# GpSimd makes two of the four sums of weights in gate and up's seven-product units; this stage's other transfers on SP's queue

## The chip, the cores and the metric

The kernel runs on one core of one Trainium2 chip. The metric is the time of one execution on the device in microseconds (us). Before the change it is 1453.75 us, the median of three runs (1453.46 to 1453.94).

The engines are TensorE (PE in the profile), VectorE (DVE), ScalarE (ACT), GpSimd (POOL) and SyncE (SP). Each runs its own instructions in order and waits for others by semaphores. DMA transfers are issued from an engine's queue: here SP's and POOL's, but for a few.

## What is computed

One encoder layer in float32, for 256 rows of 2048 features: four mixers side by side behind one input projection (gated linear attention, a Fourier mixer, a long convolution, a short convolution), an output projection, a cross-attention over 256 memory rows, and a gated feed-forward layer. The change is in the last:

```python
def swiglu(h, w_gate_up, w_down):
    gate, up = jnp.split(h @ w_gate_up, 2, axis=-1)
    return (jax.nn.silu(gate) * up) @ w_down

x = x + swiglu(rms_norm(x, norm_g[l, 2]), w_gate_up[l], w_down[l])
return rms_norm(x, final_norm_g)
```

`w_gate_up` is 2048 by 11264, `w_down` 5632 by 2048.

## The kernel before

**Weights.** All weights come as one stream of 252 slabs of 1 MB (128 partitions by 2048 columns, which are sixteen 128 by 128 blocks). `Stream.raw` (L129) loads a slab into a `raw` tile from SP's queue (L136); in gate and up there are four such tiles in turn, so that a load waits until the slab four before it has been read. To keep float32's accuracy a product is made of three matmuls of a shorter format. For that `Stream.split` (L150) divides 1024 columns at a time: ACT copies the rounded weights to `wh` (L156), DVE subtracts them from the raw ones and leaves the rest in `wl` (L157). A pair of `wh` and `wl` is called a part here. `Stream.free` (L141) allows five parts at a time in this stage (pools `wp` and `wp2`); the next part's copy waits until PE is through with the oldest one.

**A product** is `Block.part` (L494): the three matmuls of L495 (`wh` by the rounded activations), L496 (`wl` by them) and L497 (`wh` by their rest), each of 512 columns, into a PSUM bank (`pg` or `pm`).

**Gate and up** (`gate_up`, L956) loops over eleven blocks j of 512 hidden columns, and in each over eight slabs i. A slab holds two rows of blocks k (2i and 2i + 1) for gate and for up. A plain slab is two parts and eight products. Slabs 1, 3 and 5 (in block 0 slab 5 alone; `sevens`, L53) are units: seven products make what eight would (Strassen's scheme in Winograd's form), with sums of weights on one side and sums of activations, made beforehand by `left` (L966), on the other. That is 31 units in this stage. The down projection has twelve more.

**A unit's weights** are made in four parts by `Stream.make` (L161). With b11, b12, b22, b21 for the four 512-column quarters of the raw slab:

- part 0: split b11 (512 columns); then one DVE instruction of 1024 columns (L189, called through `op`) puts b11 - b12 and b22 - b12 in the places of b11 and b12;
- part 1: split b22 and b21 as loaded; then two DVE instructions of 512 columns: b22 becomes b22 + (b11 - b12), and b21 becomes b21 less the new b22;
- part 2: split the first two quarters (the sums of part 0);
- part 3: split the last two quarters (the sums of part 1).

Each sum is written into the raw tile in place. `keep` after each part (`keep_place`, L345) ties every instruction of it to the one before on the same engine, so that the scheduler can't move it past others. Parts are made ahead of their use, as far as buffers are free (`look`, L204).

**Other work of the stage.** `combine` (L995) adds a unit group's banks to the sums kept in SBUF, `finish` (L1009) adds the plain products, applies the gate and has `store_turned` (L520) transpose the result on DVE (L525) and store it to a scratch tensor `hidden` in HBM with four DMAs each (L530), eight in a block. `fetch` (L932) loads 128 hidden columns back at a time (L941) and splits them for the down projection: 16 during gate and up (`form` is None), 28 more in the down projection, where some are also formed into sums. `turn` (L1067) transposes the residual on DVE (16 times, L1074), stores it with 64 DMAs (L1077) and loads it with 8 (L1081). All these DMAs (L530, L941, L1077, L1081) are issued from POOL's queue.

**Order.** A list scheduler fixes each engine's order from the order in which the program is written down and the dependencies. The small work (`combine`, `finish`, `turn`, `fetch`) is written down by generators of the class `Background` (L244), which counts PE time (`pe`) and a debt of DVE time (`dve`, L262) in the program: `poll` lets a generator go on only while the debt is under 0.9 us.

Of the kernel before, what the change touches and what calls it, by code (L numbers as in the profile page):

```python
# [18 lines left out]
ALU = mybir.AluOpType  # L19
# [3 lines left out]
P = 128  # L23
# [88 lines left out]
class Stream:  # L112
# [48 lines left out]
    def make(self):  # L161

        nc, (slab, part) = self.nc, self.todo
        n = 16 * slab + 8 * part
        if n >= NBLK - HELD:
            parts = [(self.places.pop(0)) for _ in range(2)]
            r = self.raw(slab)[:, part * 1024:part * 1024 + 1024]
            for a, (wh, wl) in zip((0, 512), parts):
                nc.scalar.copy(wh, r[:, a:a + 512])
                nc.vector.tensor_tensor(out=wl, in0=r[:, a:a + 512], in1=wh.bitcast(F32), op=ALU.subtract)  # L170
            self.bg.dve(1024, 2)
            self.items.append((None, parts))
            self.todo = (slab + part, 1 - part)
            return True
        pool = self.free(slab)
        if pool is None:
            return False
        raw = self.raw(slab)
        at = 48 if any(a <= n < b for a, b in ROWS) else 8
        r = raw[:, part % 2 * 1024:part % 2 * 1024 + 1024]  # L180
        if not seven(slab):
            mark = len(nc.cur_bb.bb.instructions)
            self.split(pool, at, r, [0, 256, 512, 1024] if n == 0 else [0, 512, 1024] if n == 8 else [0, 1024])
            if DOWN <= slab < DOWN + 2 * AHEAD:
                self.keep(mark)
            self.todo = (slab + part, 1 - part)
            return True
        mark = len(nc.cur_bb.bb.instructions)
        op = lambda out, a, b, what=ALU.subtract: nc.vector.tensor_tensor(out=out, in0=a, in1=b, op=what)  # L189
        self.split(pool, at, r, [0, 512] if part == 0 else [0, 1024])  # L190
        b11, b12, b22, b21 = (raw[:, a:a + 512] for a in range(0, 2048, 512))
        if part == 0:
            blk = raw.rearrange("p (b c) -> p b c", b=4)
            op(r.rearrange("p (b c) -> p b c", b=2), blk[:, 0:3:2, :], blk[:, 1:2, :].to_broadcast([P, 2, 512]))
            self.bg.dve(1024)
        elif part == 1:
            op(b22, b22, b11, ALU.add)
            op(b21, b21, b22)
            self.bg.dve(1024, 2)
        self.keep(mark)  # L200
        self.todo = (slab + part // 3, (part + 1) % 4)
        return True
# [87 lines left out]
class Block:  # L290
# [226 lines left out]
                    self.bg.poll()  # L517
        return ps

    def store_turned(self, to, u, src, keep=False):  # L520

        nc = self.nc
        self.bg.dve(src.shape[1])
        mark = self.mark()
        nc.vector.transpose(u, src)  # L525
        if keep:
            self.keep_place(mark)
        to = to.rearrange("(b f) t -> f b t", f=32)
        for a in range(4):
            nc.gpsimd.dma_start(to[:, :, 32 * a:32 * a + 32],  # L530
                                u[32 * a:32 * a + 32, :].rearrange("f (b t) -> f b t", t=32))


# [398 lines left out]
    def fetch(self, f, ks, ahead, pause, form=None):  # L932

        m = {}
        for n in range(len(ks) + ahead):
            if n < len(ks):
                k = ks[n]
                while len(self.stored) <= k // 4:
                    yield
                m[k] = self.tmp()  # L940
                self.nc.gpsimd.dma_start(m[k], self.ff[k * P:(k + 1) * P, :])  # L941
            if n >= ahead:
                i = ks[n - ahead]
                if i >= PLAIN:
                    if i % 2:
                        form(i - 1, m.pop(i - 1), m.pop(i))
                        self.have += 2
                        yield 3.0
                    continue
                mark = self.mark()  # L950
                self.split(f[i], m.pop(i))
                self.keep_place(mark)
                self.have += 1
                yield pause

    def gate_up(self, sw, gp, f):  # L956
# [52 lines left out]
        def finish(j, cs, s):  # L1009
# [5 lines left out]
            for r in range(2):  # L1015
                g, h = s[r]
                self.tt(h, cs[r][1], h, ALU.add)
                yield SOON
            for r in range(2):
                g, h = s[r]  # L1020
                u = gp.tile([P, 512], F32, name="u", tag="u", bufs=2)
                self.stt(h, h, box["col"][:, r:r + 1], g, ALU.mult, ALU.mult)
                yield SOON
                self.store_turned(self.ff[j * 512:(j + 1) * 512, r * P:(r + 1) * P], u, h)
                yield SOON
            self.stored.append(j)

# [39 lines left out]
    def turn(self):  # L1067
# [3 lines left out]
        for i in range(16):  # L1071
# [2 lines left out]
            nc.vector.transpose(u, self.resk(i))  # L1074
            for a in range(4):
                c = i * P + 32 * a
                nc.gpsimd.dma_start(to[:, :, c:c + 32], u[32 * a:32 * a + 32, :].rearrange("t (b f) -> t b f", f=32))  # L1077
            yield 4.0
        for c in range(4):
            for r in range(2):  # L1080
                nc.gpsimd.dma_start(self.half(c, r), self.xr[r * P:(r + 1) * P, c * 512:(c + 1) * 512])  # L1081
            yield

    def half(self, c, r):
# [794 lines left out]
```

## Time and profile before

| | |
|---|---|
| time, median of 3 runs | 1453.75 us (1453.46 to 1453.94) |
| profiled execution, its own time | 1454.31 us |
| its span, first instruction to last | 1452.4 us |
| PE busy | 1439.1 us |
| DVE busy | 1192.3 us |
| ACT busy | 844.1 us |
| POOL busy | 172.2 us |
| granted TensorE clock | 0.998 |

In the profile an instruction's line is that of kernel.py; a line can be a helper's, as L157 for every split of weights and L189 for every sum of weights. A group's row gives count, busy time, the mean duration of one in ns, and after the bar the idle time of the engine just before it with what ended it. A wait row gives total time, count and the longest. In a windows row every engine's busy time stands for each stretch of the span, with its number of instructions in brackets. A timeline row gives start, duration, engine, line and tiles, and in brackets the idle time before it. Durations of one engine can overlap slightly, since instructions are pipelined.

### The profile page before, as it was taken

The page shows a single profiled execution, that of the slowest core. Times are in us where ns is not written, and L with a number is a line of the kernel's source. Part 1 is how long each engine was busy: PE and PEld are TensorE (multiplying, and loading weights), DVE is VectorE, ACT ScalarE, POOL GpSimd, SP SyncE. Part 2 cuts the span into 40 slices and gives each one's busy share as a digit, 9 for nine tenths or more (in the row PEclk, how much of TensorE's full clock was granted, in tenths as well). Part 3 has the DMA queues.
Part 4 walks back from the last instruction along what each step waited for, and adds up shares of the span by engine and source line. Part 5 has one row for each costly group of instructions (what it writes and reads, how often), then busy time and mean ns, then how long its engine had stood idle before and what let it go on. Part 6 is the DMA issues. An engine that isn't in the chain of part 4 may idle for free.

```text
span 1452.4 us, 19765 instructions
## 1 busy us (share of the span) xinstructions
PE 1439.1 (99%) x7231; PEld 1217.8 (84%) x7231; DVE 1192.3 (82%) x1750; ACT 844.1 (58%) x1254; POOL 172.2 (12%) x294
## 2 busy tenths in 40 slices
PE   9999999999999999999999999999999999999997
PEld 8888888898899888888888888888888888788886
DVE  6587768778868767877778999999999997988875
ACT  6565655466656646765565555555655564655554
POOL 0220100000000001100003334112111112100000
PEclk9999999999999999999999999999999999999999
DMA  9985654454535656555555767666667656655654
GB/s 352 339 289 197 220 193 168 152 187 156 195 129 206 215 179 224 172 170 195 178 205 205 277 234 243 220 209 237 233 220 250 221 200 220 214 184 199 225 203 146
DMA packets 57394, 307.17 MB, mean 211 GB/s; under 512 B 9773, under 2 KB 11470, under 8 KB 25680
## 3 DMA queue, kind: packets, MB, share of 16 engines
q1 hardware_dynamic: 45920, 281.11, 54.9%
q0 software_dynamic: 10944, 24.14, 5.4%
q8 instruction: 57, 0.93, 0.3%
q10 hardware_dynamic: 432, 0.66, 0.1%
q14 instruction: 41, 0.34, 0.1%
HBM read 291.71 MB, written 14.16 MB: 211 GB/s over the span
## 4 chain that ended last, share of the span: by engine, by line
PE 94%; DVE 2%; issue 2%; ACT 1%; DMA 1%; POOL 1%; SPq 0%; DVEq 0%; POOLq 0%; ACTq 0%
PE pg L444 19%; PE pg L496 13%; PE pg L497 13%; PE pg L495 13%; PE pg L445 10%; PE pm L496 6%; PE pm L495 6%; PE pm L497 6%; PE pm L1380 1%; DVE wl L157 1%; PE pg L441 1%; PE pg L442 1%; PE pm L895 1%; PE pm L868 1%; DMA tmp<-hidden 1%
## 5 line engine op out<-in xcount | busy, mean ns | idle before, releaser
L156 ACT CAST wh<-raw 128x1024 fp32r<-128x1024 f32 (+1 forms) x589 | 589.2, 1013 | 466.6 <-PE pg L497 149.7
L157 DVE TENSOR_TENSOR wl<-raw,wh 128x1024 fp32r<-128x1024 f32 (+1 forms) x589 | 681.4, 1175 | 177.8 <-ACT wh L156 171.7
L444 PE MATMUL pg<-act,wh 128*128 128x512 f32 x1104 | 387.5, 393 | 0.0
L445 PE MATMUL pg<-act,wl 128*128 128x256 f32 x1216 | 340.7, 280 | 0.0
L496 PE MATMUL pg<-wl,act 128*128 128x512 f32 (+1 forms) x689 | 268.3, 389 | 1.5 <-DVE wl L157 1.4
L495 PE MATMUL pg<-wh,act 128*128 128x512 f32 (+1 forms) x689 | 268.7, 391 | 0.0
L497 PE MATMUL pg<-wh,act 128*128 128x512 f32 (+1 forms) x689 | 268.3, 389 | 0.0
L444 PEld LDWEIGHTS pg<-act,wh 128*128 128x128 f32 x1104 | 207.4, 188 | 44.9
L445 PEld LDWEIGHTS pg<-act,wl 128*128 128x128 f32 x1216 | 228.5, 188 | 0.8 <-DVE wl L157 0.5
L496 PEld LDWEIGHTS pg<-wl,act 128*128 128x128 f32 x689 | 129.5, 188 | 29.6 <-DVE wl L157 3.1
L495 PEld LDWEIGHTS pg<-wh,act 128*128 128x128 f32 x689 | 129.6, 188 | 27.5 <-issue 0.8
L497 PEld LDWEIGHTS pg<-wh,act 128*128 128x128 f32 x689 | 129.4, 188 | 27.4 <-issue 0.4
L496 PE MATMUL pm<-wl,act 128*128 128x512 f32 x318 | 123.7, 389 | 0.0
L497 PE MATMUL pm<-wh,act 128*128 128x512 f32 x318 | 123.7, 389 | 0.0
L495 PE MATMUL pm<-wh,act 128*128 128x512 f32 x318 | 123.6, 389 | 0.0
L189 DVE TENSOR_TENSOR raw<-raw 128x1024 f32<-128x1024 f32 x129 | 111.7, 866 | 3.0
L530 POOL DMA_DIRECT2D hidden<-u x88 | 56.8, 653 | 162.3 <-DVE u L525 139.7
L495 PEld LDWEIGHTS pm<-wh,act 128*128 128x128 f32 x318 | 59.7, 188 | 12.5
L497 PEld LDWEIGHTS pm<-wh,act 128*128 128x128 f32 x318 | 59.7, 188 | 12.4
L496 PEld LDWEIGHTS pm<-wl,act 128*128 128x128 f32 x318 | 59.7, 188 | 12.4
L1077 POOL DMA_DIRECT2D xrows<-tmp x64 | 37.0, 586 | 182.7 <-DVE rc L323 126.6
L941 POOL DMA_DIRECT2D tmp<-hidden x44 | 24.5, 560 | 145.7 <-DVE f L319 73.4
(361 smaller groups left out, 1778.6 us busy)
## 6 DMA issues: line engine op xcount, KB each, us to landing
raw<-in_W SPq DMA_DIRECT2D x246, 1024.0 KB, 5.0
raw<-in_W SPq DMA_DIRECT2D x11, 512.0 KB, 7.5
hidden<-u POOLq DMA_DIRECT2D x88, 64.0 KB, 4.4
tmp<-hidden POOLq DMA_DIRECT2D x44, 128.0 KB, 4.6
res<-in_xT SPq DMA_DIRECT2D x8, 512.0 KB, 8.4
k<-in_mem SPq DMA_DIRECT2D x8, 256.0 KB, 6.8
k<-in_x SPq DMA_DIRECT2D x8, 256.0 KB, 9.9
keys<-k POOLq DMA_DIRECT2D x32, 64.0 KB, 5.4
```

The source lines that it names most:

```text
L156: nc.scalar.copy(wh[:, a:b], r[:, a:b])
L157: nc.vector.tensor_tensor(out=wl[:, a:b], in0=r[:, a:b], in1=wh[:, a:b].bitcast(F32), op=ALU.subtract)
L189: op = lambda out, a, b, what=ALU.subtract: nc.vector.tensor_tensor(out=out, in0=a, in1=b, op=what)
L441: self.nc.tensor.matmul(p[:, 0:R], wh, slot[:, 0:R], start=start, stop=False)
L444: self.nc.tensor.matmul(p[:, :], wh, slot[:, :], start=start, stop=False)
L445: self.nc.tensor.matmul(p[:, 0:R], wl, slot[:, 0:R], start=False, stop=stop)
L495: self.nc.tensor.matmul(p, hi, wh, start=start, stop=False)
L496: self.nc.tensor.matmul(p, hi, wl, start=False, stop=False)
L497: self.nc.tensor.matmul(p, lo, wh, start=False, stop=stop)
L530: nc.gpsimd.dma_start(to[:, :, 32 * a:32 * a + 32], u[32 * a:32 * a + 32, :].rearrange("f (b t) -> f b t", t=32))
L941: self.nc.gpsimd.dma_start(m[k], self.ff[k * P:(k + 1) * P, :])
L1077: nc.gpsimd.dma_start(to[:, :, c:c + 32], u[32 * a:32 * a + 32, :].rearrange("t (b f) -> t b f", f=32))
```

## The change

In gate and up's units (slabs before `DOWN`) the two sums of part 1 are issued to GpSimd and no longer charged to the background's debt; in the down projection's units they stay on DVE. The DMAs that stood in POOL's queue during gate and up go to SP's queue: the stores of hidden values, the 16 early fetches, the residual's stores and loads. The 28 later fetches (with `form`) stay in POOL's queue. `store_turned` has another user, the keys of the cross-attention, which stays as it was. From L198 on, lines of the changed kernel stand up to four further down.

```diff
         elif part == 1:
-            op(b22, b22, b11, ALU.add)
-            op(b21, b21, b22)
-            self.bg.dve(1024, 2)
+            if slab < DOWN:
+                nc.gpsimd.tensor_tensor(out=b22, in0=b22, in1=b11, op=ALU.add)
+                nc.gpsimd.tensor_tensor(out=b21, in0=b21, in1=b22, op=ALU.subtract)
+            else:
+                op(b22, b22, b11, ALU.add)
+                op(b21, b21, b22)
+                self.bg.dve(1024, 2)
...
-    def store_turned(self, to, u, src, keep=False):
+    def store_turned(self, to, u, src, keep=False, queue=None):
...
-            nc.gpsimd.dma_start(to[:, :, 32 * a:32 * a + 32],
+            (queue or nc.gpsimd).dma_start(to[:, :, 32 * a:32 * a + 32],
...
-                self.nc.gpsimd.dma_start(m[k], self.ff[k * P:(k + 1) * P, :])
+                (self.nc.gpsimd if form else self.nc.sync).dma_start(m[k], self.ff[k * P:(k + 1) * P, :])
...
-                self.store_turned(self.ff[j * 512:(j + 1) * 512, r * P:(r + 1) * P], u, h)
+                self.store_turned(self.ff[j * 512:(j + 1) * 512, r * P:(r + 1) * P], u, h, queue=nc.sync)
...
-                nc.gpsimd.dma_start(to[:, :, c:c + 32], u[32 * a:32 * a + 32, :].rearrange("t (b f) -> t b f", f=32))
+                nc.sync.dma_start(to[:, :, c:c + 32], u[32 * a:32 * a + 32, :].rearrange("t (b f) -> t b f", f=32))
...
-                nc.gpsimd.dma_start(self.half(c, r), self.xr[r * P:(r + 1) * P, c * 512:(c + 1) * 512])
+                nc.sync.dma_start(self.half(c, r), self.xr[r * P:(r + 1) * P, c * 512:(c + 1) * 512])
```

## Prediction

> **What bounds the kernel now.** The page's head and its slices come first.
>
> ```profile
> span 1452.4 us, 19765 instructions
> ...
> PE 1439.1 (99%) x7231; PEld 1217.8 (84%) x7231; DVE 1192.3 (82%) x1750; ACT 844.1 (58%) x1254; POOL 172.2 (12%) x294
> ...
> PE   9999999999999999999999999999999999999997
> ...
> DVE  6587768778868767877778999999999997988875
> ```
>
> TensorE (PE) is busy for 1439.1 of 1452.4 us, VectorE (DVE) for 82%. DVE's digits rise to 9 in slices 25 to 35, the gate-and-up stage that the change edits. A busy PE need not be at its peak, so the windows of this stage are read next, with their counts of matmuls.
>
> ```profile
> 800.00:900.00 100.00, 100.00 (x442) 82.79 (x442) 96.83 (x113) 56.13 (x62) 38.17 (x64) 1.00 0.74 253
> 900.00:1000.00 100.00, 100.00 (x443) 82.79 (x442) 94.20 (x107) 56.67 (x63) 19.21 (x32) 1.00 0.66 234
> 1000.00:1100.00 100.00, 100.00 (x443) 82.81 (x442) 94.89 (x111) 55.50 (x64) 21.15 (x34) 1.00 0.64 218
> 1100.00:1200.00 100.00, 100.00 (x443) 82.81 (x442) 95.44 (x108) 59.02 (x70) 13.18 (x21) 1.00 0.64 224
> 1200.00:1300.00 100.00, 97.04 (x423) 78.71 (x422) 84.04 (x130) 55.35 (x82) 16.07 (x28) 1.00 0.61 214
> ```
>
> For 400 us PE starts 442 or 443 matmuls in each 100 us, one every 0.226 us, without a gap: inside the stage nothing can be gained. In 1200:1300, where gate and up hand over to the down projection, 423 start: 20 missing, 20 x 0.226 = 4.5 us. **That is all that any relief of DVE can win.** DVE stands at 95.3% on average in the four full windows (96.83, 94.20, 94.89, 95.44), so it is close to being the bound itself. The longest of PE's own waits is one for DVE's split:
>
> ```profile
> PE pg L496 <- DVE wl L157: 1.9, 2, 1.4
> ```
>
> The timeline gives the length of one block of 512 hidden columns, by the same addition at its seam:
>
> ```profile
> 1040.07 0.69 DVE L319 TENSOR_TENSOR g<-pg,g 128x512 f32<-128x512 f32 x1 [0.24 <-PE pg L497]
> 1040.67 1.22 DVE L157 TENSOR_TENSOR wl<-raw,wh 128x1024 fp32r<-128x1024 f32 x1
> 1041.81 0.68 DVE L319 TENSOR_TENSOR g<-pg,g 128x512 f32<-128x512 f32 x1
> ...
> 1062.89 1.23 DVE L189 TENSOR_TENSOR raw<-raw 128x1024 f32<-128x1024 f32 x1
> 1064.04 1.22 DVE L157 TENSOR_TENSOR wl<-raw,wh 128x1024 fp32r<-128x1024 f32 x1
> 1065.29 1.42 DVE L189 TENSOR_TENSOR raw<-raw 128x512 f32<-128x512 f32 x2
> ...
> 1066.96 6.90 DVE L157 TENSOR_TENSOR wl<-raw,wh 128x1024 fp32r<-128x1024 f32 x6
> ...
> 1081.55 0.69 DVE L319 TENSOR_TENSOR g<-pm,g 128x512 f32<-128x512 f32 x1 [0.80 <-PE pm L497]
> ```
>
> 1081.55 - 1040.07 = 41.5 us. A block is 5 plain slabs of 24 matmuls (5.4 us) and 3 units of 21 (4.75 us). The four rows from 1062.89 are one unit's DVE work: the first sum (L189, 1024 wide), the split of part 1 (L157, 1064.04), the two sums in question (1065.29, x2), a piece of other work, and the splits of parts 2, 3 and of what follows. Consecutive starts show what an instruction occupies: 0.60 us at 512 columns, 1.14 at 1024 (1040.67 - 1040.07 and 1041.81 - 1040.67). The group rows, a little longer since instructions overlap, are:
>
> ```profile
> L157 DVE TENSOR_TENSOR wl<-raw,wh 128x1024 fp32r<-128x1024 f32 x186 | 220.8, 1216 | 9.7 <-ACT wh L156 8.7
> L189 DVE TENSOR_TENSOR raw<-raw 128x512 f32<-128x512 f32 x58 | 39.8, 686 | 1.1
> ...
> L525 DVE STREAM_TRANSPOSE u<-h 128x512 f32<-128x512 f32 x20 | 13.0, 686 | 0.0
> L323 DVE SCALAR_TENSOR_TENSOR h<-h,rc,g 128x512 f32<-128x512 f32 x18 | 12.7, 745 | 0.0
> ```
>
> **Part 1: two sums leave DVE.** In a block 3 x 2 x 0.60 = 3.6 us go. DVE's free time was 41.5 x (1 - 0.953) = 1.95 us, so it becomes 5.5 us. By itself this moves nothing, since PE has no gap there to close.
>
> **Part 2: the sums run on GpSimd (POOL).** The four parts of a unit stand one behind another on DVE and ScalarE (ACT). The sums may start when part 1's split has read the raw weights; part 3's copy on ACT, and then its split on DVE, wait for the second sum, which waits for the first. No POOL sum is in this trace. The nearest rows of this engine:
>
> ```profile
> L1077 POOL DMA_DIRECT2D xrows<-tmp x64 | 37.0, 586 | 182.7 <-DVE rc L323 126.6 <-DVE tmp L1074 53.1 <-issue 1.6
> ...
> L1580 POOL MEMSET gs<- 128x512 f32 x2 | 1.0, 526 | 123.8 <-DVE res L319 123.8
> ```
>
> A sum's price is bounded below by DVE's own 0.69 us (L189 above). Above: POOL's clearing of a tile of this shape (L1580), one stream, takes 0.526 us; a sum moves three (two in, one out), one after another 1.58 us. I take 1.58, from the only row of this engine at this shape, and keep 0.69. The Trainium skill's GPSIMD Engine Reference, section 3.1, gives 4497 ns for such an add of 2048 columns, an estimate of 1.12 us for 512, by which the waits below would be 2.5 us and fit into DVE's free time; no run here shows it yet.
>
> The wait needs the copy's and the handover's length:
>
> ```profile
> L156 ACT CAST wh<-raw 128x1024 fp32r<-128x1024 f32 x186 | 191.0, 1049 | 153.1 <-DVE raw L189 69.6 <-PE pm L497 40.8 <-PE pg L497 40.3
> L156 ACT CAST wh<-raw 128x512 fp32r<-128x512 f32 x29 | 18.0, 621 | 13.8 <-PE pm L497 7.1 <-PE pg L497 6.1
> ```
> ```profile
> 1064.23 1.05 ACT L156 CAST wh<-raw 128x1024 fp32r<-128x1024 f32 x1 [1.68 <-DVE raw L189]
> ```
>
> The copy is 1.05 us. It started 1064.23, when the sum before it had ended at 1062.89 + 1.23 = 1064.12: a handover is 0.1 us. From the end of part 1's split: 0.1 + 1.58 + 0.1 + 1.58 + 0.1 + 1.05 = 4.5 us until part 3's split can start. DVE has part 2's split (1.14) to do meanwhile, and stands for 3.4 us; it runs in order, so all later splits stand with it. In the changed order of instructions this is so for the units of slabs 3 and 5. In slab 1 the additions of the block before (two to four of 0.60 us from PSUM, two of 0.66, L323) stand in between and cover it. Two units: 6.8 us of waiting against 5.5 us free: **1.3 us too much per block**, in ten blocks (the first has one unit) 13 us. With a sum of 0.69 the wait is 1.6 us, 3.2 per block, and nothing is lost. The point where it decides is 2.75 us of wait, a sum of 1.27 us. In 800:1200 ACT also waits for PE:
>
> ```profile
> ACT wh L156 <- PE pm L497: 47.9, 41, 2.1
> ACT wh L156 <- PE pg L497: 46.4, 40, 2.1
> ```
>
> These 94 us are waits for one of the five buffers of parts; while all are full, DVE's spare time can't be stored up. So 13 us is no upper end. ACT waits behind part 3's copy too; its 56% busy time covers that.
>
> **Part 3: what is no longer charged.** The sums' 1024 columns and two instructions are not charged to the background's debt. In the changed order the 16 transposes of the residual and the 16 early fetches are through by block 5, before by block 10: the same DVE work, 1 us a block more early and 1 less late. I cost it at nothing; in the sum it only moves which blocks pay.
>
> **Part 4: transfers on SP's queue.** What SP issues in this stage is weights:
>
> ```profile
> L136 SPq DMA_DIRECT2D raw<-in_W x259: 327/328/801, 1.2 to 1421.6; - x130
> ...
> DMA to landing us min/median/max: 3.3/5.0/8.9
> ```
> ```profile
> raw<-in_W SPq DMA_DIRECT2D x246, 1024.0 KB, 5.0
> ...
> hidden<-u POOLq DMA_DIRECT2D x88, 64.0 KB, 4.4
> ```
>
> SP takes 0.33 us per issue, the weights land in a median of 5.0 us (3.3 to 8.9), a store of hidden values in 4.4 from POOL's queue. 88 stores of hidden values, 64 of the residual, 8 loads and 16 fetches now stand among the weights, and a store that waits for DVE holds every weight load behind it. How often ACT waited for weights in the whole span:
>
> ```profile
> ACT wh L156 <- DMA raw<-in_W: 5.8, 6, 2.7
> ```
>
> Six times, 5.8 us: so far they came in time. From block 4 on the order puts eight stores once a block, behind loads that were issued far ahead; 8 x 0.33 = 2.6 us are hidden. **In block 2 they are not.** There the weights of slab 2 stand behind 8 residual stores and both groups of hidden stores, and DVE makes the second group's input late. From the end of block 1 on PE: last addition 0.60, two products 1.32 (L323 and L525 less the 0.08 of overlap), split of part 0 0.60, transpose 0.61, first sum 1.14, split 1.14, transpose 0.61 = 6.0; four issues 1.3; the load 5.0; copy 1.05; split 1.22: 14.6 us. PE wants it after a plain slab and a unit, 5.4 + 4.75 = 10.2 us: 4.4 us late (2.7 with the fastest landing). Block 3 has the like ahead of slab 3, where the load also waits for the first store's landing. Part 3 of its first unit gets its buffer 12 matmuls into the block, 2.7; copy 1.05, split 1.14, two products 1.32, transpose 0.61, landing 4.4, load 5.0, copy and split of 512 columns 0.62 and 0.69: 17.5, wanted after 5.4 + 4.75 + 5.4 = 15.6, so 1.9 late, or none with a fast landing. Together 6.3 us, from 2.7 up. An issue of such a small-pieced store on SP is in no row; POOL's took 0.65 of its own time, and at that price eight more cost 2.6 us, still covered but for blocks 2 and 3.
>
> **Part 5: the seam to the down projection.** Two timeline rows, POOL's and ACT's:
>
> ```profile
> 1213.22 5.16 POOL L530 DMA_DIRECT2D hidden<-u  x8 [9.39 <-DVE u L525]
> ```
> ```profile
> 1249.62 0.41 ACT L327 CAST act<-tmp 128x256 fp32r<-128x256 f32 x1 [4.04 <-DMA tmp<-hidden]
> ```
>
> POOL issued the last hidden stores in one run of 5.2 us with fetches behind them, and ACT stood 4.0 us for a fetch. Eight stores leave POOL's queue, and eleven of the 28 late fetches move ahead of the last sums. What stays is DVE's own pile of splits and forms there. I take half of the 4.5 us, 2.2, from 0 to 4.5.
>
> **The sum.** The profiled execution took 1454.3 us (span 1452.4, about 2 around it), 0.6 above the median of the runs, 1453.75. 1454.3 + 13 + 6.3 - 2.2 = 1471.4; I say **1471**.
>
> **Rivals.**
> - *The sums fit.* A sum of 1.27 us or less leaves only the late weights and the seam: 1454.3 + 6.3 - 2.2 = 1458.4, with the bounds 1452.5 (2.7 and the whole seam) to 1463 (2.6 for dear issues, no seam). For it: DVE's sum is 0.69 us and POOL's one stream 0.53. Against: ACT and DVE wait in order, so that every handover counts.
> - *Faster: the seam closes.* The sums fit, weights come in time because DVE, 3.6 us a block lighter, has made the transposes earlier than I lay them out, and the whole seam is won: 1454.3 - 4.5 = 1449.8. Its place is 1200:1300, its price 4.5 us, and it decides at a sum of 1.27 us and a weight load of block 2 issued within 2.9 us of the block's start (10.2 - 5.0 - 1.05 - 1.22). For it: the 20 missing matmuls; against: in block 2 the transposes stand behind additions that need the end of block 1.
> - *DVE and POOL shut each other out.* Both read weight tiles at the same time. If one engine's two-input instruction keeps the other's waiting, a unit's part 2 split and the two sums run one after another: the wait grows by 1.14 us. At 1.58 it is 4.5, 9.0 a block, 3.5 too much, 35 in all: 1454.3 + 35 + 6.3 - 2.2 = 1493.4; at 0.69 it is 2.75, just at the limit. In these rows POOL issues DMAs in 0.586 us beside a busy DVE (L1077), which speaks against it, but these read no tile. The rule is in the Trainium skill, SBUF — State Buffer, "Who interferes with whom": a DVE instruction with two SBUF inputs contends with a GpSimd one that reads SBUF, and the later one blocks in full; no run here shows it yet. By it and the 1.12 us above the wait would be 3.6 us, near my forecast by another way.
>
> **How the numbers follow.** Forecast 50% (1460 to 1485 alone), the sums fit 22%, the seam 18%, shut out at the high price 10%. A difference under 0.2% (2.9 us) can't be told from none: 1450.8 to 1456.7. The forecast and the last rival are slower; of "the sums fit" 13% lie above, 9% within. Faster 18%, same 9%, slower 73%. The range, 1449.5 to 1485, takes in the faster end and leaves out the last rival.
>
> **What would show it.** POOL's rows for the sums: 1.6 us means my price, about 1.1 with DVE's splits lengthened or POOL late means shutting out, under 1.27 and no idle DVE before part 3 means that they fit. Right: in 1000:1200 fewer than 443 matmuls per 100 us, PE waiting for L157, DVE idle behind ACT's copy and that behind POOL. In blocks 2 and 3 (835 to 920 us before) ACT should wait for the weight DMA. At the seam: 423 matmuls or more. It is wrong if 443 stay in every window, or if small stores on SP take well over 0.65 us to issue, which would make every block's weights late.

## The result, and the profile after

| | before | after |
|---|---|---|
| median of 4 runs each, in turn on one chip | 1453.85 us (1453.46 to 1454.11) | 1499.63 us (1498.19 to 1500.93) |
| span of the profiled execution | 1452.4 us | 1496.1 us |

The ratio is 1.0314, with a 95% interval of 1.0301 to 1.0327: 45.8 us slower. The forecast had 1471 and a range up to 1485, so the sign was right and the size far too small. The head of the page after, and DVE's slices:

```profile
span 1496.1 us, 19780 instructions
...
PE 1455.0 (97%) x7231; PEld 1216.8 (81%) x7231; DVE 1163.9 (78%) x1688; ACT 839.2 (56%) x1254; POOL 173.2 (12%) x180
...
DVE  6687869779768778777698785888778787888875
```

The work is the same: PE has its 7231 matmuls, and DVE is 28 us less busy (1192.3 before). But PE is now busy for 97% of its span instead of 99%. The windows of the stage, in the form shown of before (PE's busy time and count, PEld, DVE, ACT, POOL, then the granted clock):

```profile
800.00:900.00 100.00, 91.92 (x387) 72.76 (x387) 80.52 (x91) 47.12 (x56) 21.08 (x12) 0.98 0.58 183
900.00:1000.00 100.00, 89.40 (x367) 69.30 (x366) 76.53 (x85) 49.57 (x63) 21.91 (x12) 0.97 0.68 235
1000.00:1100.00 100.00, 96.27 (x416) 77.36 (x415) 79.92 (x84) 50.63 (x56) 27.25 (x18) 1.00 0.65 211
1100.00:1200.00 100.00, 97.72 (x426) 79.24 (x425) 81.35 (x85) 53.67 (x59) 28.80 (x21) 1.00 0.65 218
1200.00:1300.00 100.00, 95.36 (x411) 76.22 (x410) 78.73 (x105) 51.60 (x73) 19.86 (x23) 1.00 0.61 207
```

No window has its 442 or 443 matmuls any more. 800:1000 is the worst (387 and 367, 131 missing), then the loss gets smaller (27 and 17 missing in the next two; the last window now lies mostly before the seam). DVE stands at 77 to 81% in all five: the bound now lies in waits, not in DVE's work. The groups of DVE and POOL, and the waits, in 800:1200:

```profile
L157 DVE TENSOR_TENSOR wl<-raw,wh 128x1024 fp32r<-128x1024 f32 x166 | 202.1, 1243 | 69.8 <-ACT wh L156 68.8
```
```profile
L198 POOL TENSOR_TENSOR raw<-raw 128x512 f32<-128x512 f32 x26 | 51.8, 1993 | 298.3 <-DVE wl L157 298.3
L199 POOL TENSOR_TENSOR raw<-raw 128x512 f32<-128x512 f32 x26 | 41.5, 1595 | 2.0
```
```profile
ACT wh L156 <- POOL raw L199: 83.4, 26, 3.8
DVE wl L157 <- ACT wh L156: 77.5, 28, 8.7
...
ACT wh L156 <- DMA raw<-in_W: 15.9, 3, 12.2
```

The first sum takes 1.99 us on average, the second 1.60. ACT waits for POOL 26 times, 83.4 us in all, and DVE for ACT 77.5 us. ACT also waits three times for weights, 15.9 us, which it did not do in this stretch before.

Where the time went shows best by blocks. A block's length here is the time from PE's first matmul on its `wl` (L496 before, L500 after) to the same of the next block; the last column is what follows block 10, up to the end.

| block | 1 | 2 | 3 | 4 | 5 | 6 | 7 | 8 | 9 | 10 | rest |
|---|---|---|---|---|---|---|---|---|---|---|---|
| before | 41.5 | 41.5 | 41.5 | 41.5 | 41.5 | 41.5 | 41.5 | 41.5 | 41.5 | 41.5 | 244.3 |
| after | 44.3 | 49.7 | 54.8 | 46.3 | 45.5 | 43.9 | 42.9 | 42.8 | 42.8 | 43.2 | 246.7 |

Blocks 7 to 10 lose 1.3 to 1.7 us each, what part 2 of the prediction gave for each of ten blocks. Blocks 2 and 3 lose 8.2 and 13.3, blocks 4 to 6 lose 4.8, 4.0 and 2.4, and what follows loses 2.4.

### The profile page after: what moved, and what is told of

Read it like the earlier page. It is cut to its first block, busy times and chain, and to the rows that moved or that the text cites. A ratio compares the mean times of both kernels' runs of the same rounds, so it can differ in the third digit from the quotient of the medians.

```text
span 1496.1 us, 19780 instructions
## 1 busy us (share of the span) xinstructions
PE 1455.0 (97%) x7231; PEld 1216.8 (81%) x7231; DVE 1163.9 (78%) x1688; ACT 839.2 (56%) x1254; POOL 173.2 (12%) x180
## 5 line engine op out<-in xcount | busy, mean ns | idle before, releaser
L500 PE MATMUL pg<-wl,act 128*128 128x512 f32 (+1 forms) x689 | 270.2, 392 | 4.2 <-DVE wl L157 4.2
L500 PEld LDWEIGHTS pg<-wl,act 128*128 128x128 f32 x689 | 129.8, 188 | 34.9 <-DVE wl L157 8.4
L500 PE MATMUL pm<-wl,act 128*128 128x512 f32 x318 | 124.5, 392 | 3.3 <-DVE wl L157 3.3
L198 POOL TENSOR_TENSOR raw<-raw 128x512 f32<-128x512 f32 x31 | 60.4, 1949 | 485.0 <-DVE wl L157 345.4
L500 PEld LDWEIGHTS pm<-wl,act 128*128 128x128 f32 x318 | 59.8, 188 | 17.4 <-DVE wl L157 5.0
L189 DVE TENSOR_TENSOR raw<-raw 128x1024 f32<-128x1024 f32 (+1 forms) x67 | 69.1, 1031 | 1.8
L199 POOL TENSOR_TENSOR raw<-raw 128x512 f32<-128x512 f32 x31 | 48.8, 1574 | 2.4
L323 DVE TENSOR_TENSOR tmp<-pg,tmp 128x256 f32<-128x256 f32 x78 | 32.4, 417 | 3.0 <-ACT tmp L455 2.2
```

The lines of the kernel that those rows point to most:

```text
L198: nc.gpsimd.tensor_tensor(out=b22, in0=b22, in1=b11, op=ALU.add)
L199: nc.gpsimd.tensor_tensor(out=b21, in0=b21, in1=b22, op=ALU.subtract)
L323: self.nc.vector.tensor_tensor(out=out, in0=a, in1=b, op=op)
L500: self.nc.tensor.matmul(p, hi, wl, start=False, stop=False)
```

## One unit in the profile after

The timeline of an ordinary unit, DVE first, then POOL and ACT:

```profile
1100.90 2.50 DVE L157 TENSOR_TENSOR wl<-raw,wh 128x1024 fp32r<-128x1024 f32 x2
1107.04 1.23 DVE L157 TENSOR_TENSOR wl<-raw,wh 128x1024 fp32r<-128x1024 f32 x1 [3.63 <-ACT wh L156]
```
```profile
1102.20 2.35 POOL L198 TENSOR_TENSOR raw<-raw 128x512 f32<-128x512 f32 x1 [7.69 <-DVE wl L157]
1104.63 1.29 POOL L199 TENSOR_TENSOR raw<-raw 128x512 f32<-128x512 f32 x1
```
```profile
1105.95 2.94 ACT L156 CAST wh<-raw 128x1024 fp32r<-128x1024 f32 x3 [3.81 <-POOL raw L199]
```

DVE splits parts 1 and 2 from 1100.90 to 1103.40; the second of the two, part 2's, begins at 1102.18. POOL's first sum starts at 1102.20, just behind it, and takes 2.35 us. The second starts at 1104.63, when DVE has nothing to do, and takes 1.29. ACT's copy of part 3 then starts at 1105.95, and DVE has stood for 3.63 us. Prediction and trace agree on the wait (3.4 and 3.63), but not on its inside: one sum is 1.29 us, less than the 1.58 taken, and the first is held until DVE's split is over at 1103.40, so that it ends 1.15 later. The split hides none of the sums: 1.15 + 0.08 + 1.29 + 0.03 + 1.05 and a handover make the 3.63.

This is so in the whole stage: a sum that starts while DVE is in a split ends 1.14 to 1.17 us after that split. It goes the other way too: where the sum starts first, the split that follows ends 1.08 us after the sum (in block 3 the sum ran from 889.22 to 890.53, and the split that began at 890.21 took 1.40 us instead of 1.22).

## The experiments

**Theory A** after this reading: the wait costs 1.3 us a block, 13 us in all; the rest comes from weights that stand behind stores on SP's queue, from background work that comes earlier, and from the seam. **Theory B**: POOL and DVE shut each other out, and that makes nearly all of it. A third, **O**, came up on the way: the scheduler had put matmuls in another order. Medians of the kernel before were 1453.3 to 1454.1 in the runs below; ratios are against those runs.

### e1_sums_alone: the sums without the queues

Against the kernel before: the change's first hunk alone, every DMA left on POOL's queue.

```diff
-            op(b22, b22, b11, ALU.add)
-            op(b21, b21, b22)
-            self.bg.dve(1024, 2)
+            if slab < DOWN:
+                nc.gpsimd.tensor_tensor(out=b22, in0=b22, in1=b11, op=ALU.add)
+                nc.gpsimd.tensor_tensor(out=b21, in0=b21, in1=b22, op=ALU.subtract)
...
```

> The two sums on GpSimd, every transfer left on GpSimd's queue. Theory A (late weights): in the profile after, a block without late weights is 42.8 us against 41.5, 1.3 us a block or 13 us in ten, and the other 31 us of the 43.7 come from transfers that hold weight loads on SP's queue, from background work and from the seam; so 1454 + 13 = 1467, up to 1475 if sums stand behind stores on GpSimd's queue. Theory B (shut out): the exclusion of GpSimd and VectorE makes nearly all of the 45 us, and the queues nothing: 1495 or more. In both, GpSimd's first sum 2.35 us and second 1.29 in slabs 3 and 5.

Measured: 1478.9 us, ratio 1.0169 (1.0154 to 1.0184). Neither number: 25 us, twice theory A's 13, little more than half of B's.

### e2_dmas_alone: the queues without the sums

Against the changed kernel: its first hunk taken back.

```diff
-            if slab < DOWN:
-                nc.gpsimd.tensor_tensor(out=b22, in0=b22, in1=b11, op=ALU.add)
-                nc.gpsimd.tensor_tensor(out=b21, in0=b21, in1=b22, op=ALU.subtract)
...
+            op(b22, b22, b11, ALU.add)
+            op(b21, b21, b22)
+            self.bg.dve(1024, 2)
```

> The transfers on SP's queue, all sums on VectorE. Theory A: VectorE is as full as before and the weights of blocks 2 and 3 come as late as in the profile after (8.2 and 13.3 us less 1.3 each, about 19): 1454 + 19 = 1473, up to 1480 with block 1. Theory B: the queues cost nothing without the waits of the sums: 1453 to 1457.

Measured: 1467.0 us, ratio 1.0090 (1.0073 to 1.0107). Theory B's "the queues cost nothing" falls; A's size is 6 us too large. Of ACT's waits in 750:1250:

```profile
ACT wh L156 <- DMA raw<-in_W: 7.4, 1, 7.4
```

One wait for weights, 7.4 us, in block 3, which is 46.9 us long. Block 9 has 45.9 us without such a wait: there PE stood 2.45 us for a split on DVE. The two halves alone make 25 + 13 = 38 us, the change 45.8: 8 us come only when they meet.

### e3_charged: the background at its old pace

Against the changed kernel:

```diff
             if slab < DOWN:
+                self.bg.dve(1024, 2)
                 nc.gpsimd.tensor_tensor(out=b22, in0=b22, in1=b11, op=ALU.add)
```

> The changed kernel with the sums' columns still charged to the background's debt, as before. Theory A: background work keeps its old pace, blocks 4 to 6 lose the 7 us that they have above 1.3 each (4.8, 4.0 and 2.4 in the profile): 1499.6 - 7 = 1492. Rival: the early pace of the background is not what costs in blocks 4 to 6, and later stores of the residual hold weights in later blocks instead: 1500, or above.

Measured: 1491.3 us, ratio 1.0259 (1.0243 to 1.0274), 8.3 us less than the change, where A had 7. Blocks 4 to 6 are 42.2, 43.0 and 43.2 us, but blocks 8 to 10 now have 44.0, 45.6 and 46.7: the last of the residual's stores (L1082 of this kernel) goes out at 1192.8 instead of 893.9.

### e4_residual_back: the residual's transfers off SP

Against the changed kernel:

```diff
-                nc.sync.dma_start(to[:, :, c:c + 32], u[32 * a:32 * a + 32, :].rearrange("t (b f) -> t b f", f=32))
+                nc.gpsimd.dma_start(to[:, :, c:c + 32], u[32 * a:32 * a + 32, :].rearrange("t (b f) -> t b f", f=32))
...
-                nc.sync.dma_start(self.half(c, r), self.xr[r * P:(r + 1) * P, c * 512:(c + 1) * 512])
+                nc.gpsimd.dma_start(self.half(c, r), self.xr[r * P:(r + 1) * P, c * 512:(c + 1) * 512])
```

> The changed kernel with the residual's 64 stores and 8 loads back on GpSimd's queue; hidden values and early fetches stay on SP's. Theory A: the weights of blocks 2 and 3 no longer stand behind stores of 0.8 us each; 15 to 20 us of the 20.5 above 1.3 a block in blocks 1 to 3 go: 1480 to 1485, if sums don't wait behind these stores on GpSimd. Theory B: 1499, nothing moves.

Measured: 1481.4 us, ratio 1.0191 (1.0176 to 1.0206). The residual's 72 transfers on SP cost 18.2 us. Blocks 2 and 3 fall from 49.7 and 54.8 us to 44.7 and 45.6. No wait of ACT for weights is left in 750:1250.

### e5 to e7: is it the order of the matmuls?

In e1 the scheduler had moved matmuls on later weights ahead of earlier ones. Three kernels (e1, e2 and the changed one) tie each matmul of the stage to the one before it, in `part` (L494), while `gate_up` runs:

```diff
+        mark = self.mark()
         self.nc.tensor.matmul(p, hi, wh, start=start, stop=False)
         self.nc.tensor.matmul(p, hi, wl, start=False, stop=False)
         self.nc.tensor.matmul(p, lo, wh, start=False, stop=stop)
+        if self.pinned:
+            self.keep_place(mark)
```

> The sums alone on GpSimd (transfers on GpSimd's queue), with TensorE's matmuls of gate and up tied in the order in which they are written down. Without the tie the scheduler had put matmuls of later weights ahead of earlier ones at ten places of this stage, and the blocks with the largest loss (46.3, 48.3, 46.4 and 44.9 us) have such places with a gap of 2.5 to 2.8 us and half the pace behind it. Theory O (order): these four blocks fall to about 42.5, so 1479 - 16 = 1463. Rival W (the waits of the sums alone): the gaps come from late weights whatever TensorE's order, 1477 to 1480.

> The transfers alone on SP's queue, sums on VectorE, with TensorE's order tied as in the run before. Theory O: the 5.4 us of block 3 and 4.4 of block 9 came from the order of matmuls, and 1467 falls to 1455 to 1458. Rival (late weights): ACT's wait of 7.4 us for a weight load in block 3 stays, and with it some 5 us there: 1462 or above.

> The changed kernel with TensorE's order tied in gate and up. There the scheduler had moved matmuls at three places of the stage (820, 844 and 911 us). Theory O: a few us in blocks 2 and 3, 1499.6 - 5 = 1494 or less. Rival: the weights are late by themselves, 1498 to 1500.

Measured: the sums alone, tied, 1493.9 us (1.0282, 1.0267 to 1.0298), 15 us slower than untied. The transfers alone, tied, 1466.5 (1.0090, 1.0075 to 1.0105), as untied. The changed kernel, tied, 1499.0 (1.0313, 1.0297 to 1.0328), unchanged. **Theory O falls**: the other order costs nothing in the changed kernel, and without it the sums alone are slower. POOL's timeline in the tied e1 shows what the sums meet when the transfers stay on POOL's queue:

```profile
904.63 1.67 POOL L949 DMA_DIRECT2D tmp<-hidden  x3 [3.92 <-DMA hidden<-u]
906.32 1.29 POOL L198 TENSOR_TENSOR raw<-raw 128x512 f32<-128x512 f32 x1
```

The first sum (L198) stands behind fetches (L949), the first of which had waited 3.92 us for a store to land. So on POOL's queue the transfers can hold the sums, on SP's the weights; how much of e1's 25 us comes from that was not separated.

### e8_charged_residual_back: both undone

Against the changed kernel: the diffs of e3 and e4 together.

```diff
             if slab < DOWN:
+                self.bg.dve(1024, 2)
...
-                nc.sync.dma_start(to[:, :, c:c + 32], u[32 * a:32 * a + 32, :].rearrange("t (b f) -> t b f", f=32))
+                nc.gpsimd.dma_start(to[:, :, c:c + 32], u[32 * a:32 * a + 32, :].rearrange("t (b f) -> t b f", f=32))
...
```

> The changed kernel with the sums charged to the background's debt and the residual's stores and loads back on GpSimd's queue (hidden values and early fetches stay on SP's). If the two parts add up: 1499.6 - 8.3 - 18.2 = 1473. If both work on the same blocks: 1478 to 1481, no more than the residual alone gave (1481.4).

Measured: 1476.2 us, ratio 1.0157 (1.0140 to 1.0174). Between the two guesses: beside e4 the charge is worth 5.2 us (1481.4 - 1476.2). Its blocks 2 to 10 are even, 42.9 to 45.3 us, 43.6 on average. What is left, 22.7 us, is the price of the sums, with hidden values and early fetches on SP.

### e9_one_input: a shorter split beside the sums

Against e8, in `split`; `one` is set for part 2 of gate and up's units alone, where the kernel leaves out the subtraction of `wh`:

```diff
+            if one:
+                nc.vector.tensor_scalar(out=wl[:, a:b], in0=r[:, a:b], scalar1=0.001, scalar2=None, op0=ALU.mult)
+            else:
...
```

> The kernel before this one (sums charged, residual back on GpSimd's queue: 1476.2) with part 2's split in gate and up's units reading one tensor of SBUF instead of two: wl is 0.001 times the raw weights, and the subtraction of wh is left out there. Theory S (shut out): in the profile GpSimd's first sum takes 2.35 us beside part 2's split and 1.29 beside nothing; with one input it takes 1.29, VectorE's wait falls from 3.63 to about 2.5 plus what the split itself gets shorter, and two waits of 2.5 fit into the 5.5 us that are free in a block: 1455 to 1460. Rival P (price): a first sum simply costs 2.35 us because of its wait or its operands: 2.35 stays, and the time with it, 1474 to 1477, less what a shorter split gives.

Measured: 1461.6 us, ratio 1.0058 (1.0044 to 1.0072). A unit of it, DVE and POOL:

```profile
1141.90 0.69 DVE L158 TENSOR_SCALAR wl<-raw 128x1024 fp32r<-128x1024 f32 x1
1146.22 2.36 DVE L160 TENSOR_TENSOR wl<-raw,wh 128x1024 fp32r<-128x1024 f32 x2 [3.63 <-ACT wh L156]
```
```profile
1142.07 1.66 POOL L202 TENSOR_TENSOR raw<-raw 128x512 f32<-128x512 f32 x1 [6.93 <-DVE wl L160]
1143.81 1.29 POOL L203 TENSOR_TENSOR raw<-raw 128x512 f32<-128x512 f32 x1
```

The split (L158) takes 0.69 us instead of 1.22. The first sum is not 1.29, as S had it, nor 2.35, as P had it, but 1.66: it ends at 1143.73, 1.14 after the split's end at 1142.59, as it does with the longer split (1104.55, 1.15 after 1103.40). So a sum's work begins when DVE's instruction is over, and rival P falls. But this split of one input shuts POOL out too, so the run doesn't show what no exclusion would give, and DVE's wait is again 3.63. The 14.6 us that the run is faster fit the shorter split by itself: 3 units by 0.53 us by ten blocks are 16, so the time alone fits P's allowance as well as S. A wait that starts at the end of DVE's last split doesn't care how long that split is.

### e10_slab1: only the units that the additions cover

Against e8:

```diff
-            if slab < DOWN:
+            if slab < DOWN and slab % 8 == 1:
```

> Sums on GpSimd only in the units of slab 1, those of slabs 3 and 5 on VectorE; hidden values and early fetches on SP's queue, the residual on GpSimd's, background charged throughout. Theory A: the additions of the block before cover the wait in slab 1, and the stores and fetches on SP cost nothing from block 4 on, so that the 22 us of the kernel with all sums go: 1454 to 1457. Rival: GpSimd's sums lengthen VectorE's instructions in slab 1 by up to 1 us a unit, and the eight stores hold weights now and then: 1460 or above.

Measured: 1456.6 us, ratio 1.0025 (1.0015 to 1.0034). Blocks 2 to 10 are 41.5 us, as before. A unit of slab 1, POOL and DVE:

```profile
1042.55 1.29 POOL L199 TENSOR_TENSOR raw<-raw 128x512 f32<-128x512 f32 x1 [28.52 <-DVE wl L157]
1043.92 2.23 POOL L200 TENSOR_TENSOR raw<-raw 128x512 f32<-128x512 f32 x1
```
```profile
1042.33 0.68 DVE L324 TENSOR_TENSOR g<-pg,g 128x512 f32<-128x512 f32 x1
...
1043.77 1.23 DVE L157 TENSOR_TENSOR wl<-raw,wh 128x1024 fp32r<-128x1024 f32 x1 [0.16 <-ACT wh L156]
...
1045.51 1.85 DVE L328 SCALAR_TENSOR_TENSOR h<-h,rc,g 128x512 f32<-128x512 f32 x2
1047.28 1.21 DVE L157 TENSOR_TENSOR wl<-raw,wh 128x1024 fp32r<-128x1024 f32 x1
```

Here the first sum runs beside additions that take one input from PSUM (L324, from 1042.33 on) and takes 1.29 us; the second is beside part 2's split (1043.77) and takes 2.23. Part 3's split follows at 1047.28 without a wait. The two products (L328, two tiles of SBUF each) take 1.85 us where they take 1.41 with POOL idle (895.03 in the profile after, shown below). Slabs 3 and 5 thus cost 1476.2 - 1456.6 = 19.6 us. Of the 3.3 us that are left, the profiles show 2.3 in their spans, and 1.9 of these behind the blocks (246.2 us after block 10, before 244.3):

```profile
1100.00:1200.00 100.00, 100.00 (x443) 82.83 (x442) 93.32 (x104) 59.18 (x69) 12.39 (x14) 1.00 0.72 243
1200.00:1300.00 100.00, 95.42 (x414) 76.86 (x413) 82.92 (x128) 54.75 (x81) 10.73 (x20) 1.00 0.60 208
```

443 matmuls in 1100:1200, but 414 in 1200:1300, where the kernel before had 423.

### e11_last_stores: the seam by itself

Against the kernel before, with the change's `queue` argument of `store_turned`:

```diff
-                self.store_turned(self.ff[j * 512:(j + 1) * 512, r * P:(r + 1) * P], u, h)
+                self.store_turned(self.ff[j * 512:(j + 1) * 512, r * P:(r + 1) * P], u, h, queue=nc.sync if j == DFF // 512 - 1 else None)
```

> The kernel before the change with one thing of it: the last block's eight stores of hidden values go out on SP's queue, all else as before. At the seam ACT stood 4.0 us for a fetch behind these stores on GpSimd's queue and PE missed 20 matmuls, 4.5 us. If that queue sets the seam: 1450 to 1452. If VectorE's pile of work does: 1453.5 to 1454.5. If the stores hold the down projection's weights instead: 1455 or above.

Measured: 1456.5 us, ratio 1.0023 (1.0013 to 1.0033).

```profile
1200.00:1300.00 100.00, 96.33 (x417) 77.52 (x416) 83.51 (x128) 54.87 (x81) 10.92 (x20) 1.00 0.62 214
```

417 matmuls instead of 423: eight stores of the last block on SP make the seam worse, and their 3.2 us are about all that e10 lost. All kernels here agree: what follows block 10 takes 242.5 to 244.9 us where these stores are on POOL's queue, 245.1 to 246.7 where they are on SP's.

### e12_stores_no_wait: the wait or the issue?

Against the changed kernel:

```diff
-                nc.sync.dma_start(to[:, :, c:c + 32], u[32 * a:32 * a + 32, :].rearrange("t (b f) -> t b f", f=32))
+                nc.sync.dma_start(to[:, :, c:c + 32], self.resk(i)[32 * a:32 * a + 32, :].rearrange("t (b f) -> t b f", f=32))
```

> The changed kernel with the residual's 64 stores taken from the untransposed residual, which lies ready, so that they wait for nothing on VectorE; the transposes still run, and what is stored is not transposed. All 72 transfers stay on SP's queue. Theory W (the wait in the queue): the weights are late because a store that waits for a transpose holds them: close to the kernel with the residual off SP, 1481 to 1486. Rival I (the issues): SP's own time, 64 issues of 0.3 to 1.6 us, holds them: 1496 to 1500.

Measured: 1478.9 us, ratio 1.0179 (1.0165 to 1.0193), 20.7 us less than the change with the same 64 stores on the same queue. But the stores, which no longer are of transposed data, now go out from 681 to 794 us, in the changed kernel from 758.6 to 894.4. So the run takes away the wait and with it their place among the weights of blocks 2 and 3, and does not test SP's own time there alone. The changed kernel's trace speaks for the wait. SP's own waits there, 750:1250:

```profile
SPq L534 <- DVE u L529: 30.4, 12, 11.7
SPq L1081 <- DVE tmp L1078: 26.1, 8, 5.8
```

SP stood 26.1 us for the residual's transposes and 30.4 for those of the hidden values; issuing one of the 64 stores took it 0.45 us in the median. And ahead of block 3's late load (shown below) the last residual stores are issued by 894.4, while the next store waits for a transpose until 897.09: there their issues hold up nothing.

### e13 to e15: what was still open

e13_slab1_old_queue, against the kernel before: the sums as in e10, every DMA left on POOL's queue.

```diff
...
+            if slab < DOWN and slab % 8 == 1:
+                self.bg.dve(1024, 2)
+                nc.gpsimd.tensor_tensor(out=b22, in0=b22, in1=b11, op=ALU.add)
+                nc.gpsimd.tensor_tensor(out=b21, in0=b21, in1=b22, op=ALU.subtract)
...
```

e14_uncharged, against the kernel before:

```diff
-            self.bg.dve(1024, 2)
+            if slab >= DOWN:
+                self.bg.dve(1024, 2)
```

e15_slabs_1_5, against e10:

```diff
-            if slab < DOWN and slab % 8 == 1:
+            if slab < DOWN and slab % 8 != 3:
```

> Sums on GpSimd only in slab 1's units, every transfer on GpSimd's queue as before, background charged. If the sums of slab 1 are covered and the 3.3 us of the kernel with hidden values on SP came from those transfers: 1452.5 to 1454.5. If sums stand behind stores on GpSimd's queue, or lengthen VectorE's work: 1456 or above.

> The kernel before with one thing of the change: in gate and up the two sums (still on VectorE) aren't charged to the background's debt, so that transposes and fetches come earlier. Theory A: VectorE had about 2 us free in a block, 1 us more of early work fits, and nothing is lost without the sums' waits: 1453 to 1455. Rival: the early pace costs wherever VectorE is full for some blocks: 1457 to 1462, the 5 to 8 us that it cost in the changed kernel.

> Sums on GpSimd in the units of slabs 1 and 5, those of slab 3 on VectorE; hidden values and early fetches on SP's queue, the residual on GpSimd's, background charged. One uncovered wait of 3.63 us a block stands against VectorE's 1.95 us free, 2.4 us of four sums gone, less about 0.4 of lengthened work in slab 1: 3.95. Theory A (the sum of free time): nothing lost in the blocks, 1456 to 1458 as with slab 1 alone. Rival: idle time can't be stored in five buffers, so that a wait costs even where the block's sum is even: 1461 or above, about half of the 19.6 us that slabs 3 and 5 cost together.

Measured: e13 1454.4 us (1.0003, 0.9994 to 1.0012), e14 1454.9 (1.0005, 0.9996 to 1.0014): neither can be told from before. e15 1460.3 (1.0043, 1.0028 to 1.0058), between both theories. So the covered sums are free, and e10's loss came from transfers on SP. The early pace of the background is free too, as long as nothing else takes DVE's time; beside the sums it costs 5 us. And one uncovered wait a block costs 3.7 us (1460.3 - 1456.6) where its block has time enough by the sum, two cost 19.6. e15's windows:

```profile
900.00:1000.00 100.00, 100.00 (x442) 82.70 (x442) 88.61 (x97) 55.46 (x63) 23.44 (x20) 1.00 0.72 236
1100.00:1200.00 100.00, 99.07 (x435) 81.04 (x434) 88.94 (x96) 55.16 (x65) 21.88 (x20) 1.00 0.70 229
```

442 matmuls in one and 435 in the other, with DVE at 89% in both. This fits a wait that costs a little before DVE's time is used up and in full after; no run varies the free time alone. No part of the change that was run by itself made the kernel faster.

## Why the prediction came out too low

| term of the sum | forecast | measured by |
|---|---|---|
| sums on POOL (part 2) | +13 | 19.6, slabs 3 and 5: e8 less e10 |
| background not charged (part 3) | 0 | 5.2 beside the sums: e4 less e8; 1.1 or nothing alone: e14 |
| weights behind transfers (part 4) | +6.3 | 18.2: the change less e4 |
| seam (part 5) | -2.2 | +3.3: e10 less before |
| sum | +17 | +46.3, against 45.8 for the change |

The measured terms are the steps of one chain (the change, e4, e8, e10, before), so their sum must come out, but for the differences between the medians of the kernel before. What belongs to each depends on the order: the charge is worth 8.3 us with the residual on SP (e3) and 5.2 without.

**Part 1** held: DVE was relieved, and by itself that gave nothing (e13). DVE's nines stand in slices 23 to 33 and in 35 of the page before, not from 25 on; nothing hangs on it.

**Part 2** was right in its mechanism and place: slabs 3 and 5 wait, slab 1 is covered (e10, e13; not in block 2 of the change, see below), the wait is 3.63 us against 3.4. Its price of 1.58 for a sum was too high (1.29), and the 1.14 that part 2's split was to hide of it was not hidden; the two errors nearly cancel. Its "1.3 us too much per block" is what blocks 7 to 9 show, in part by luck: the last early fetch had gone out at 965, so that DVE had less to do there. Over all ten it is 2.0 (19.6), as the free time of 5.5 us was smaller than summed: products and splits in slab 1 last longer beside the sums, and 0.23 us a wait was missing, 4.6 us over twenty waits.

**Part 3**, "I cost it at nothing", failed. The reason given, that the same work is only moved, holds where DVE has room (e14). It had none left: part 2 had just spent it.

**Part 4** is the largest error. The step "In block 2 they are not" (hidden), with its sum "Together 6.3 us, from 2.7 up", named the right places, blocks 2 and 3, and the right cause, weights behind a store that waits for a transpose, but 18.2 us came of it. Two things in it failed.

First, it priced a late weight at its lateness alone. In block 2 of the changed kernel the load goes out 8.1 us into the block (7.3 in the prediction). PE's gaps for it add up to 2.9 us (4.4 in the prediction, 2.7 at the least), but matmuls at half pace behind them (last section) cost 1.6 more. The rest of the 8.2 that the block loses are waits for sums: 2.5 in slab 1, which was not covered here, and 1.1 in a later unit. e2 shows a late weight without the sums. Its block 3 starts at 879.1; SP's, ACT's and PE's rows:

```profile
890.00 2.11 SPq L136 DMA_DIRECT2D raw<-in_W  x4
```
```profile
895.77 1.57 ACT L156 CAST wh<-raw 128x512 fp32r<-128x512 f32 x2 [7.38 <-DMA raw<-in_W]
```
```profile
894.66 0.39 PE L497 MATMUL pm<-wh,act 128*128 128x512 f32 x1
896.44 0.50 PE L495 MATMUL pg<-wh,act 128*128 128x512 f32 x1 [1.39 <-ACT wh L156]
...
899.58 0.80 PE L495 MATMUL pg<-wh,sh 128*128 128x512 f32 x1 [1.24 <-ACT wh L156]
```

The load goes out 10.9 us into the block and PE comes to its gap at 15.6, both near the prediction's layout (11.2 and 15.6; in part by luck, as DVE's order was another). The gap of 1.78 us is near its 1.9 too. But the slab is a unit, made in parts one behind another: PE stands again for the next part, up to 899.58, and then runs five matmuls at half pace. The block loses 5.4 us. (Block 2 of e2 loses nothing, where the prediction had 4.4.)

Second, with the sums the weight itself comes later. Block 3 of the changed kernel starts at 887.3; SP's, DVE's and ACT's rows:

```profile
888.01 6.36 SPq L1081 DMA_DIRECT2D xrows<-tmp  x8
897.09 4.41 SPq L534 DMA_DIRECT2D hidden<-u  x8
901.60 0.43 SPq L136 DMA_DIRECT2D raw<-in_W  x1
```
```profile
890.21 1.40 DVE L157 TENSOR_TENSOR wl<-raw,wh 128x1024 fp32r<-128x1024 f32 x1
...
893.89 1.23 DVE L157 TENSOR_TENSOR wl<-raw,wh 128x1024 fp32r<-128x1024 f32 x1 [0.75 <-ACT wh L156]
895.03 1.41 DVE L327 SCALAR_TENSOR_TENSOR h<-h,rc,g 128x512 f32<-128x512 f32 x2
896.36 1.30 DVE L529 STREAM_TRANSPOSE u<-h 128x512 f32<-128x512 f32 x2
```
```profile
892.81 2.94 ACT L156 CAST wh<-raw 128x1024 fp32r<-128x1024 f32 x3 [1.75 <-POOL raw L199]
907.91 1.56 ACT L156 CAST wh<-raw 128x512 fp32r<-128x512 f32 x2 [12.16 <-DMA raw<-in_W]
```

The prediction laid out the transpose for which the first hidden store waits to end 6.8 us into the block (2.7 + 1.05 + 1.14 + 1.32 + 0.61). It ended at 897.06, 9.8 into it: part 3's split (893.89) stands in DVE's order ahead of the products (895.03) and the transposes (896.36), and its copy on ACT (892.81) came 2.8 us later than laid out. Of these ACT had waited 1.75 us for POOL's second sum; the rest are two activations on ACT, until 891.06, that the prediction's chain left out. The sums so reach block 3's stores through slab 1, where the prediction had called the wait covered (DVE stood 0.75 us for the copy). The eight hidden stores are then issued in 4.41 us, where the prediction had the first one's landing, 4.4, and the weight load goes out at 901.60, 14.3 us into the block (11.2 in the prediction). ACT's copy of it starts 6.3 us later, at 907.91 (5.0 in the prediction), when ACT has stood 12.16 us. PE's gaps up to the first matmuls on it come to 5.3 us instead of 1.9, that for the unit's next part to 1.1, half pace to 1.8. The rest of the block's 13.3 are the sums' waits in slabs 3 and 5, 3.5, and a late split on DVE ahead of them, 1.4. The chains of blocks 2 and 3 were laid out with DVE and ACT on time, while the same text made them late by the sums' waits: the terms were added as if each met a kernel without the others. Without the sums all the moved transfers together cost 13 us (e2); with them the residual's alone cost 18.2.

**Part 5** had the wrong sign. Moving stores off POOL's queue didn't close the seam, and on SP they opened it further: 3.2 us for the last block's eight alone (e11). What in it holds PE was not settled: DVE's pile, or the down projection's weights that stand behind the stores.

**The signs and the rivals.** The signs in gate and up came: fewer than 443 matmuls, DVE idle behind ACT's copy and that behind POOL, ACT waiting for weights in blocks 2 and 3. The one at the seam did not, and neither did a sign of being wrong: small stores on SP took 0.49 us (hidden values) and 0.45 us (residual) to issue in the median, not well over 0.65. "The sums fit" and "the seam closes" fell with the price of 3.63 for a wait. "DVE and POOL shut each other out" named what the traces show inside the wait: a sum of 2.35 us beside the split, 1.29 without. The rule of the Trainium skill, SBUF — State Buffer, "Who interferes with whom", agrees with the traces in this. But the rival's 1493.4 was made with a sum of 1.58, and its 35 us for the waits are not what was measured; it came near by the wrong terms. The Trainium skill's GPSIMD Engine Reference, section 3.1, had led to an estimate of 1.12 us for a sum; the trace has 1.29.

## What to carry to other kernels

Where one engine is 95% busy, its free time is a purse from which every part of a change is paid: add the parts' costs against what is left, not each against the whole (nothing that could be measured, and 5.2 us, for the same edit). An engine given work that another then waits for, in order, helps only where other work covers the wait; two of three units here had none. And before a store is put into a queue of loads, ask what the store waits for: here 72 transfers on the loads' queue cost 18 us, and the trace shows the waits behind it rather than the issues.

## What the runs showed of the hardware beyond that

Where PE had stood for some 2 us, its matmuls often ran at about half pace for a while. PE's rows in block 2 of the changed kernel, and the window around them:

```profile
849.89 0.40 PE L501 MATMUL pg<-wh,act 128*128 128x512 f32 x1
852.09 0.73 PE L499 MATMUL pg<-wh,act 128*128 128x512 f32 x2 [1.80 <-ACT wh L156]
...
854.80 0.63 PE L499 MATMUL pg<-wh,act 128*128 128x512 f32 x1
855.23 0.63 PE L500 MATMUL pg<-wl,act 128*128 128x512 f32 x1
```
```profile
850.00:860.00 10.00, 7.67 (x26) 5.65 (x25) 6.55 (x6) 4.61 (x5) 2.42 (x2) 0.83 1.03 405
```

2.20 us lie between the starts at 849.89 and 852.09. Soon after, matmuls follow one another by 0.43 us (854.80, 855.23) instead of 0.227, eight in a row until 857.3, and the granted clock of the window is 0.83. Eight times 0.2 is 1.6 us beside the gap itself. The changed kernel has two such stretches, which cost 3.4 us, the tied e1 six, which cost 9.3. Each of these followed gaps of 2.2 us or more; in e2 gaps of 1.8 and 1.6 us within 5 us were enough, and in e8 once two of 1.2 and 1.3 us in a row (857 us). The changed kernel's single gaps of 1.3 us, one a unit, did not do it, and neither did a single one of 2.24 at 825 us. So no threshold comes out of these runs. The Trainium skill, TensorE: Matmul & The Clock Gate, Part 1, gives half the clock after an idle window of about 3.4 us; here shorter gaps were enough, with matmuls between them. The prediction had priced a late weight at its lateness alone.
